# An encoder kernel in split float32: up projections by Strassen's seven products on halves

## The chip, the cores and the metric

The kernel runs on one core of a Trainium2 chip, in one launch. The core's engines are TensorE (PE: matmuls; PEld: their weight loads), VectorE (DVE), ScalarE (ACT), GpSimd (POOL) and SyncE (SP, which issues most DMAs). The metric is the device time in microseconds: the median of three runs before the change is 2168.96, from 2166.63 to 2170.75.

## The reference

Two layers of an encoder on 512 tokens with 1024 channels, followed by a last RMSNorm. Each layer is

```
x += 0.5 * swiglu(rms_norm(x, g1), Wgate1, Wup1, Wdown1)
z = rms_norm(x, gmix) @ W_in                # four mixers: neighbourhood, sliding-window,
y = concat of rms_norm of the 4 mixers      # latent and dilated attention
x += y @ W_out
x += 0.5 * swiglu(rms_norm(x, g2), Wgate2, Wup2, Wdown2)
x += sigmoid(rms_norm(x, gple) @ Wg) * (p @ Wp)

swiglu(u, Wgate, Wup, Wdown) = (silu(u @ Wgate) * (u @ Wup)) @ Wdown     # 1024 -> 2816 -> 1024
```

Everything is float32. There are four feed-forwards (two per layer), and the change is in them.

## The kernel before, in words

Activations lie with channels on the 128 partitions and the 512 tokens along the free axis, so x is eight tiles `x0` to `x7` of 128x512. A float32 product is done in three matmuls of a faster format: each operand is split into a high half, rounded to that format, and a low half, the rest (`split` for activations, lines 115 to 124; `pieces`, from line 150 on, for weights). `mm3y` (lines 194 to 203) issues, for each 128 rows of the contraction, high x high, high x low and low x high into one PSUM bank.

Weights come in tiles of 128x1024 (eight 128x128 blocks), 512 KB each, loaded by SP into `raw` (two buffers). A tile is cut in two pieces of four blocks: ACT writes the high half `wh` (L173) and DVE, in the mixers POOL, the low half `wl` (L175); each has three buffers. `plan` lists all weight tiles of the program in the order of use, and `take` hands out the next piece and prepares one more ahead. PE's and SP's instructions stand in the order in which the program writes them; the order of the other engines is laid out by a scheduler when the program is built, and is then fixed.

A feed-forward (`ffn`) has 22 gate tiles and 22 up tiles of 128 output channels, in two blocks of 11. Per tile f, `ffn` issues the gate's two pieces (24 matmuls of 512 columns into a bank `ps`), the up's two pieces (24 into a bank `s`), and `gated`: DVE multiplies the gate by the token's scale `rb`, ACT takes tanh, DVE makes silu (L276), multiplies by up (L277), and ACT and DVE split the result into `hs`. After a block follow eight down tiles with 8 + 3 blocks each, and DVE adds them to x (L316, L317). In the second block each finished x tile goes through `feed`: ACT and DVE write the split of x times the norm's gain (`act`, L122, L123) for the next stage, ACT squares x and POOL adds the squares (L216). The scale itself (`rstat`, `rspread`: four narrow matmuls, DVE, POOL, four transposes) is asked for after the first gate and up tile.

A mixer ends in `out` (inside `mix`): eight output tiles, each added to x by DVE (L779) and fed. The last part of a layer, `ple`, ends in the same way with `ple_out` (L821 to L824).

Of the kernel before, what the change touches and what calls it, by code (L numbers as in the profile page):

```python
# [16 lines left out]
D = 1024  # L17
T = 512
KC = 8
FF = 22  # L20
HF = 11
# [13 lines left out]
class Encoder:  # L35
# [34 lines left out]

    def dense(self):
        return self.ps.tile([128, T], F32, tag="ps", name=self.nm("ps"), bufs=3)
# [8 lines left out]
    def setup(self):  # L81
# [8 lines left out]
        self.supply = self.pieces()  # L90
# [35 lines left out]
    def plan(self):  # L126
        a = self.a
        full = ((0, 4, 128), (512, 4, 128))
        for l in range(self.depth):
            for w in range(2):  # L130
                for half in range(2):
                    for f in range(HF):
                        for i in range(2):
                            yield a["ffn_gu"][l, w, half * HF + f, i], full
                    for m in range(KC):
                        yield a["ffn_d"][l, w, half, m][:, 0:8], full
                        yield a["ffn_d"][l, w, half, m][:, 8:HF], ((0, 3, 128),)
                if w == 0:
                    for i in range(M_END):
                        if i == M_DQ0:  # L140
                            for j in range(2):
                                yield a["w_up"][l, j], ((0, 2, 256), (512, 1, 256))
                        yield a["w_in"][l, i], full
                    for i in range(8):
                        yield a["w_out"][l, i], full
            for m in range(KC):
                yield a["ple"][l, m][:, 0:4], ((0, 4, 128),)
                yield a["ple"][l, m][:, 4:10], ((0, 3, 128), (384, 3, 128))

    def pieces(self):  # L150
        nc, a = self.nc, self.a
        first = True
        for src, cuts in self.plan():
            n = cuts[-1][0] + cuts[-1][1] * cuts[-1][2]
            raw = self.tile("raw", [128, 1024], F32, 2)
            src = src.rearrange("p k m -> p (k m)") if len(src.shape) == 3 else src
            if first:
                nc.sync.dma_start(raw[:, :512], src[:, :512])
                nc.sync.dma_start(self.x[0], a["x"][:, 0])
                nc.sync.dma_start(self.x[1], a["x"][:, 1])  # L160
                nc.sync.dma_start(self.x[2], a["x"][:, 2])
                nc.sync.dma_start(raw[:, 512:], src[:, 512:])
                for k in range(3, KC):
                    nc.sync.dma_start(self.x[k], a["x"][:, k])
                first = False
            else:
                nc.sync.dma_start(raw[:, :n], src)
            for o, k, m in cuts:
                c = k * m
                hi = self.tile("wh", [128, 512], F32R, 3)[:, :c]  # L170
                lo = self.tile("wl", [128, 512], F32R, 3)[:, :c]
                r = raw[:, o:o + c]
                nc.scalar.activation(hi, r, AF.Copy)  # L173
                eng = nc.gpsimd if self.mixing else nc.vector
                eng.tensor_tensor(out=lo, in0=r, in1=hi.bitcast(F32), op=ALU.subtract)  # L175
                yield (hi.rearrange("p (k m) -> p k m", k=k), lo.rearrange("p (k m) -> p k m", k=k))

    def take(self):
# [3 lines left out]
        if not self.ready:  # L182
            self.prep()
        return w

    def prep(self):
        w = next(self.supply, None)
        if w is not None:
            self.ready.append(w)
# [56 lines left out]
    def begin(self, l, off):  # L246
        self.norm = (l, off)
        self.nacc = self.acc()
        self.xn = []

    def feed(self, m, square=True):
# [3 lines left out]
        if l < self.depth:  # L255
# [9 lines left out]

    def squared(self, m):
# [3 lines left out]
    def gated(self, gp, up, rb, h):  # L270
# [6 lines left out]
        nc.vector.tensor_tensor(gr, gr, up, op=ALU.mult)  # L277
        self.split(h, gr)

    def ffn(self, l, w, nxt):  # L280
        nc, a = self.nc, self.a
        xs, acc, rb = self.xn, self.nacc, None
        for half in range(2):
            hs = [self.big() if f < 6 else self.keep() for f in range(HF)]
            held = None
            for f in range(HF):
# [693 lines left out]
```

## Time and profile before

| | |
|---|---|
| median of 3 runs | 2168.96 us (2166.63 to 2170.75) |
| span of the profiled execution, first to last instruction | 2163.3 us |
| time of that execution beside its span | not given; the median lies 5.7 us above the span |
| instructions | 25721 |
| PE, PEld, DVE, ACT, POOL busy | 98%, 79%, 56%, 43%, 13% |
| DMA | 195.38 MB, mean 90 GB/s |
| mean granted clock of TensorE | 0.994 of 2.4 GHz |

Busy times of PE are modelled: a matmul of 512 columns is shown with 0.39 us, though the next one starts 0.23 us after it. So paces are read from the starts of successive instructions in the timeline, not from the durations. On DVE and ACT, too, a following instruction can start a little before the one ahead has ended.

### The profile page before, as it was taken

How to read it: one execution, taken by the hardware profiler on the slowest of the kernel's cores; microseconds unless marked ns; L12 is line 12 of the kernel's file. 1: busy time of each engine (PE TensorE's matmuls, PEld its weight loads, DVE VectorE, ACT ScalarE, POOL GpSimd, SP SyncE). 2: the span in 40 equal slices, each digit the busy share in tenths (PEclk: the TensorE clock that was granted, in tenths of full speed). 3: DMA queues.
4: the chain of work that ended last, by engine and by line, in shares of the span. 5: the costliest groups of instructions: out<-in, count | busy, mean ns of one | idle time of the engine just before them, and what ended most of it. 6: DMA issues, size and time to landing. Idle time of an engine off the chain costs nothing.

```text
span 2163.3 us, 25721 instructions
## 1 busy us (share of the span) xinstructions
PE 2117.2 (98%) x9564; PEld 1718.6 (79%) x9564; DVE 1210.5 (56%) x1926; ACT 930.1 (43%) x1690; POOL 280.0 (13%) x230
## 2 busy tenths in 40 slices
PE   8999999999999999999999999999999999999997
PEld 6888888677778888888888888886777788888886
DVE  5444446567766444456654444555687654444554
ACT  4332334477754332333533233345677533233343
POOL 2000001444321000001100000025332200000011
PEclk9999999999999999999999999999999999999998
DMA  3232223212112222223322322232121122322322
GB/s 129 97 109 99 98 94 111 90 60 75 40 54 93 98 96 99 98 98 96 100 96 98 94 102 98 93 102 93 64 59 49 59 98 98 94 101 98 102 92 89
DMA packets 63358, 195.38 MB, mean 90 GB/s; under 512 B 7552, under 2 KB 15872, under 8 KB 63232
## 3 DMA queue, kind: packets, MB, share of 16 engines
q1 hardware_dynamic: 61808, 187.92, 26.0%
q0 software_dynamic: 1280, 5.77, 1.0%
q8 instruction: 75, 1.23, 0.2%
q14 instruction: 51, 0.42, 0.1%
q10 hardware_dynamic: 144, 0.05, 0.0%
HBM read 189.51 MB, written 2.10 MB: 89 GB/s over the span
## 4 chain that ended last, share of the span: by engine, by line
PE 92%; DVE 4%; ACT 2%; issue 1%; DMA 1%; POOL 0%; POOLq 0%; SPq 0%; DVEq 0%; ACTq 0%
PE ps L200 15%; PE ps L201 15%; PE ps L202 15%; PE s L201 13%; PE s L200 13%; PE s L202 13%; PE pv L455 2%; PE s L439 2%; PE s L398 2%; PE s L397 1%; DVE kl L343 1%; PE s L225 1%; PE s L236 0%; ACT tmp L326 0%; DVE PT L443 0%
## 5 line engine op out<-in xcount | busy, mean ns | idle before, releaser
L173 ACT ACTIVATE wh<-raw 128x512 fp32r<-128x512 f32 (+1 forms) x712 | 437.8, 615 | 971.2 <-PE ps L201 457.3
L175 DVE TENSOR_TENSOR wl<-raw,wh 128x512 fp32r<-128x512 f32 (+1 forms) x614 | 435.6, 710 | 405.6 <-ACT wh L173 399.0
L200 PE MATMUL ps<-act,wh 128*128 128x512 f32 x616 | 248.8, 404 | 6.1 <-ACT act L122 6.1
L216 POOL TENSOR_TENSOR acc<-acc,tmp 128x512 f32<-128x512 f32 x54 | 72.3, 1340 | 1365.4 <-ACT tmp L215 1365.0
L200 PE MATMUL ps<-big,wh 128*128 128x512 f32 x616 | 247.0, 401 | 0.0
L201 PE MATMUL ps<-act,wh 128*128 128x512 f32 x616 | 242.7, 394 | 3.3 <-DVE act L123 3.1
L202 PE MATMUL ps<-act,wl 128*128 128x512 f32 x616 | 242.1, 393 | 0.0
L202 PE MATMUL ps<-big,wl 128*128 128x512 f32 x616 | 240.6, 391 | 0.0
L201 PE MATMUL ps<-big,wh 128*128 128x512 f32 x616 | 240.3, 390 | 0.0
L200 PE MATMUL s<-act,wh 128*128 128x512 f32 x520 | 202.4, 389 | 0.0
L200 PE MATMUL s<-big,wh 128*128 128x512 f32 x520 | 202.4, 389 | 0.0
L202 PE MATMUL s<-act,wl 128*128 128x512 f32 x520 | 202.3, 389 | 0.0
L202 PE MATMUL s<-big,wl 128*128 128x512 f32 x520 | 202.3, 389 | 0.0
L201 PE MATMUL s<-big,wh 128*128 128x512 f32 x520 | 202.3, 389 | 0.0
L201 PE MATMUL s<-act,wh 128*128 128x512 f32 x520 | 202.3, 389 | 0.0
L175 POOL TENSOR_TENSOR wl<-raw,wh 128x512 fp32r<-128x512 f32 (+1 forms) x98 | 127.4, 1300 | 286.6 <-ACT wh L173 286.4
L200 PEld LDWEIGHTS ps<-act,wh 128*128 128x128 f32 x616 | 116.7, 189 | 30.1 <-ACT act L122 6.4
L201 PEld LDWEIGHTS ps<-act,wh 128*128 128x128 f32 x616 | 116.7, 189 | 28.5 <-DVE act L123 7.3
L202 PEld LDWEIGHTS ps<-act,wl 128*128 128x128 f32 x616 | 116.6, 189 | 24.6
L202 PEld LDWEIGHTS ps<-big,wl 128*128 128x128 f32 x616 | 115.7, 188 | 24.7
L200 PEld LDWEIGHTS ps<-big,wh 128*128 128x128 f32 x616 | 116.0, 188 | 23.5 <-issue 1.1
L201 PEld LDWEIGHTS ps<-big,wh 128*128 128x128 f32 x616 | 116.2, 189 | 21.4
(172 smaller groups left out, 3373.1 us busy)
## 6 DMA issues: line engine op xcount, KB each, us to landing
raw<-in_ffn_gu SPq DMA_DIRECT2D x175, 512.0 KB, 3.5
raw<-in_ffn_d SPq DMA_DIRECT2D x64, 512.0 KB, 3.4
raw<-in_w_in SPq DMA_DIRECT2D x40, 512.0 KB, 3.5
raw<-in_ffn_d SPq DMA_DIRECT2D x64, 192.0 KB, 2.5
raw<-in_w_out SPq DMA_DIRECT2D x16, 512.0 KB, 3.5
raw<-in_ple SPq DMA_DIRECT2D x16, 384.0 KB, 3.0
raw<-in_ple SPq DMA_DIRECT2D x16, 256.0 KB, 2.6
nb<-in_na_bias POOLq DMA_DIRECT2D x8, 448.0 KB, 4.1
```

The costliest lines, as they stand in the source:

```text
L173: nc.scalar.activation(hi, r, AF.Copy)
L175: eng.tensor_tensor(out=lo, in0=r, in1=hi.bitcast(F32), op=ALU.subtract)
L200: nc.tensor.matmul(ps, lhsT=wh[:, k], rhs=x[:, 0], start=start and k == 0, stop=False)
L201: nc.tensor.matmul(ps, lhsT=wh[:, k], rhs=x[:, 1], start=False, stop=False)
L202: nc.tensor.matmul(ps, lhsT=wl[:, k], rhs=x[:, 0], start=False, stop=stop and k == last)
L216: eng.tensor_tensor(out=acc, in0=acc, in1=sq, op=ALU.add)
L225: nc.tensor.matmul(ss[:, t:t + 1], lhsT=acc[:, t * 128:(t + 1) * 128], rhs=self.ones, start=True, stop=True)
L343: nc.vector.tensor_tensor(out=kl[r], in0=u[r], in1=t[r, e].bitcast(F32), op=ALU.subtract)
L397: nc.tensor.matmul(s, lhsT=q[:, e, qs], rhs=k[0][:, e, k0:k1], start=True, stop=False)
L398: nc.tensor.matmul(s, lhsT=q[rows, e, qs], rhs=k[1][rows, k0:k1], start=False, stop=True)
L439: nc.tensor.transpose(tp[:, t * 128:(t + 1) * 128], h["P"][t][:, o:o + 128], self.ident)
L455: nc.tensor.matmul(pv[:, c], lhsT=vb, rhs=h["pt"][b][:, i, c], start=b == 0 and i == 0, stop=b == 3 and i == 1, skip_group_check=True)
```

## The change

For two neighbouring up tiles (an "up pair", 256 output channels) and the 512 tokens, the product W^T x is cut in halves in three directions: the eight tiles of x in those with even and odd number, the output channels in two tiles, the tokens in two halves of 256. Strassen's scheme in the variant with seven products then needs sums of weight halves (`factors`: four sums on DVE per pair), sums of activation halves (`combos`: made once per feed-forward, for each two x tiles, and split like the others into `pp` tiles), seven products (`product`: 4 x 3 matmuls of 256 columns each) and additions of the results. X1 to X4 add into one PSUM bank, Z1 and Z2 into another, Y is alone; after each step `seven` reads the bank on ACT or DVE into the up tiles `u`. `feed` writes x times gain first (ACT, L307 of the changed kernel) and splits that.

`ORDER` says how the pair's seven pieces (s) and the two gate tiles' four pieces (d) follow one another; the first pair of a feed-forward has `ORDER0`, and there the scale is asked for after the first two gate pieces. Two pieces instead of one are prepared ahead in the feed-forwards. Blocks are 12 and 10 tiles, so the down tiles have 8 + 4 and 8 + 2 blocks. `raw` has four buffers, which now hold the tables and biases of the mixers as well, and the mixers' P and PT lie in `pp`.

```diff
-HF = 11
+HT = 256
+CUT = (0, 12, 22)
+S_STEPS = ("X1", "Z1", "X2", "Y", "X3", "Z2", "X4")
+ORDER, ORDER0 = "ssdssdssdsd", "ddssdssdsss"
...
+                    for f in range(c0, c1, 2):
+                        gu = a["ffn_gu"][l, w]
+                        s = self.factors(gu[f, 1], gu[f + 1, 1])
+                        d = self.slices((gu[f, 0], full), (gu[f + 1, 0], full))
+                        for c in ORDER if f else ORDER0:
+                            yield s if c == "s" else d
...
+    def factors(self, src1, src2):
+        a, b = self.load(src1), self.load(src2)
+        a11, a12, a21, a22 = a[:, 0:512], a[:, 512:1024], b[:, 0:512], b[:, 512:1024]
...
+        yield self.cut(a11, 4)
+        s1 = plus(a21, a22)
+        yield self.cut(s1, 4)
+        s2 = plus(s1, a11)
+        yield self.cut(s2, 4)
+        yield self.cut(a12, 4)
+        yield self.cut(plus(a11, a21), 4)
+        yield self.cut(plus(s2, a12), 4)
+        yield self.cut(a22, 4)
...
+            nc.scalar.activation(xg, self.x[m], AF.Copy, scale=self.g(l, off, m))
+            self.split(t, xg)
+            if m % 2:
+                self.tn.append(self.combos(self.xg))
...
+        nc.vector.tensor_tensor(out=f[:, 0:2], in0=q[:, 0::3], in1=q[:, 1:2].to_broadcast([128, 2, HT]),
+                                op=ALU.subtract)
+        nc.vector.scalar_tensor_tensor(f[:, 2], f[:, 0], -1.0, q[:, 3], op0=ALU.mult, op1=ALU.subtract)
+        nc.vector.scalar_tensor_tensor(f[:, 3], f[:, 2], -1.0, q[:, 2], op0=ALU.mult, op1=ALU.subtract)
+        for i in (0, 2):
+            t = self.pp().rearrange("p e (h t) -> p e h t", h=2)
+            nc.scalar.activation(t[:, :, 0], f[:, i:i + 2], AF.Copy)
+            nc.vector.tensor_tensor(out=t[:, :, 1], in0=f[:, i:i + 2], in1=t[:, :, 0].bitcast(F32), op=ALU.subtract)
...
+    def product(self, ps, w, right, start):
+        nc = self.nc
+        wh, wl = w
+        for k, x in enumerate(right):
+            for i, (v, e) in enumerate(((wh, 0), (wh, 1), (wl, 0))):
+                nc.tensor.matmul(ps, lhsT=v[:, k], rhs=x[:, e], start=start and k == i == 0,
+                                 stop=k == 3 and i == 2, skip_group_check=True)
...
+            self.product(ps, self.take(), self.right(name, xs, tn), name in ("X1", "Y", "Z1"))
+            if name == "X1":
+                nc.scalar.activation(u[:, 0, lo], ps, AF.Copy)
+            elif name == "Z1":
+                nc.scalar.activation(u[:, 1, hi], ps, AF.Copy, scale=-1.0)
+            elif name == "X2":
+                nc.scalar.activation(u[:, 0, hi], ps, AF.Copy)
+            elif name == "Y":
+                nc.vector.tensor_tensor(u[:, 0, lo], u[:, 0, lo], ps, op=ALU.add)
+            elif name == "X3":
+                nc.vector.tensor_tensor(u[:, 1, hi], u[:, 1, hi], ps, op=ALU.subtract)
+            elif name == "Z2":
+                nc.vector.tensor_tensor(u[:, 0, hi], u[:, 0, hi], ps, op=ALU.add)
+            else:
+                nc.scalar.activation(u[:, 1, lo], ps, AF.Copy, scale=-1.0)
...
-            raw = self.tile("raw", [128, 1024], F32, 2)
+        return self.tile("raw", [128, 1024], F32, 4)
...
-        p = self.tile("P", [128, T], F32, 8)
+        if t % 2 == 0:
+            h["Pp"] = self.pp(F32)
+        p = h["Pp"][:, t % 2]
...
-        pt = self.tile("PT", [128, 2, T], F32R, 3)
+        pt = self.pp()
...
-            nb = self.tile("nb", [128, 896], F32, 1)
+            nb = self.raw()[:, :896]
...
-        cos = self.tile("tab", [128, T], F32, 2)
-        sin = self.tile("tab", [128, T], F32, 2)
+        tab = self.raw()
+        cos, sin = tab[:, :T], tab[:, T:]
```

On PE, in an up tile before: two blocks of the contraction, three matmuls of 512 columns each (`s` is the up's bank, `act` the split x).

```order
L200 MATMUL s97_522<-act8_112,wh95_506 128x512
L201 MATMUL s97_522<-act8_112,wh95_506 128x512
L202 MATMUL s97_522<-act8_112,wl96_507 128x512
L200 MATMUL s97_522<-act11_119,wh98_523 128x512
L201 MATMUL s97_522<-act11_119,wh98_523 128x512
L202 MATMUL s97_522<-act11_119,wl99_524 128x512
```

And in the changed kernel, the first product of a pair, X1, and the start of Z1 (`pp` holds the split sums of activations; "x2" are two matmuls with the same weights):

```order
L369 MATMUL s387_2031<-act5_103,wh370_1983 128x256 x2
L369 MATMUL s387_2031<-act5_103,wl371_1984 128x256
L369 MATMUL s387_2031<-act11_122,wh370_1983 128x256 x2
L369 MATMUL s387_2031<-act11_122,wl371_1984 128x256
L369 MATMUL s387_2031<-act19_145,wh370_1983 128x256 x2
L369 MATMUL s387_2031<-act19_145,wl371_1984 128x256
L369 MATMUL s387_2031<-act25_164,wh370_1983 128x256 x2
L369 MATMUL s387_2031<-act25_164,wl371_1984 128x256
L369 MATMUL s391_2051<-pp9_116,wh373_2001 128x256 x2
L369 MATMUL s391_2051<-pp9_116,wl374_2002 128x256
L369 MATMUL s391_2051<-pp15_135,wh373_2001 128x256 x2
L369 MATMUL s391_2051<-pp15_135,wl374_2002 128x256
```

The same contraction now passes in seven shorter runs of 256 columns, each with its own cut weights.

On DVE, inside a block before: cuts of weights (L175) alternate with the gating (L273, L276, L277, L120).

```order
L273 TENSOR_TENSOR tmp404_2172<-ps392_2102,rb49_260 128x512
L175 TENSOR_TENSOR wl403_2157<-raw401_2154,wh402_2156 128x512
L276 SCALAR_TENSOR_TENSOR tmp404_2172<-tmp405_2174,tmp404_2172 128x512
L175 TENSOR_TENSOR wl408_2182<-raw401_2154,wh407_2181 128x512
L277 TENSOR_TENSOR tmp404_2172<-tmp404_2172,s398_2137 128x512
L175 TENSOR_TENSOR wl411_2200<-raw409_2197,wh410_2199 128x512
L120 TENSOR_TENSOR keep277_1475<-tmp404_2172,keep277_1475 128x512
L175 TENSOR_TENSOR wl414_2217<-raw409_2197,wh413_2216 128x512
```

And in the changed kernel, at the place where a pair's last pieces meet the next pair's sums. `wl399` is the cut of the second half of gate tile `raw388`; `raw417` and `raw418` are the next pair's two up tiles, and `raw418` is loaded into the buffer of `raw388` after that cut; L212 are the sums, L390 and L392 read PSUM, L354 is the gating's first product, and `wl411` and `wl413` are cuts that this pair still needs.

```order
L197 TENSOR_TENSOR wl399_2089<-raw388_2032,wh398_2088 128x512
L197 TENSOR_TENSOR wl403_2109<-y401_2106,wh402_2108 128x512
L390 TENSOR_TENSOR keep386_2030<-keep386_2030,ps400_2105 128x256
L197 TENSOR_TENSOR wl406_2128<-y404_2125,wh405_2127 128x512
L212 TENSOR_TENSOR y421_2225<-raw418_2206 128x512
L212 TENSOR_TENSOR y432_2273<-y421_2225,raw417_2204 128x512
L212 TENSOR_TENSOR y441_2327<-raw417_2204,raw418_2206 128x512
L354 TENSOR_TENSOR tmp407_2143<-ps395_2071,rb70_310 128x512
L212 TENSOR_TENSOR y444_2346<-y432_2273,raw417_2204 128x512
L197 TENSOR_TENSOR wl411_2151<-raw409_2148,wh410_2150 128x512
L392 TENSOR_TENSOR keep386_2030<-keep386_2030,s387_2031 128x256
L197 TENSOR_TENSOR wl413_2168<-raw369_1981,wh412_2167 128x512
```

The four sums of the next pair now stand ahead of a cut of this pair, and the first of them needs a tile whose load is issued four rows earlier.

On DVE at the end of the first mixer, before: the last two x tiles are added (L779), a weight piece is cut, and the splits' low halves are written (L123).

```order
L779 TENSOR_TENSOR x6_78<-x6_78,ps1213_5521 128x512
L175 TENSOR_TENSOR wl1237_5584<-raw1219_5546,wh1236_5583 128x512
L123 SCALAR_TENSOR_TENSOR act1216_5539<-x6_78,gain_70,act1216_5539 128x512
L779 TENSOR_TENSOR x7_79<-x7_79,s1218_5545 128x512
L175 TENSOR_TENSOR wl1240_5602<-raw1238_5599,wh1239_5601 128x512
L123 SCALAR_TENSOR_TENSOR act1222_5565<-x7_79,gain_70,act1222_5565 128x512
L216 TENSOR_TENSOR acc1189_5410<-acc1189_5410,tmp1223_5568 128x512
```

And in the changed kernel, from the last add to x (L914) to the low half of x7 (`act1350`); L326, L328, L329 and L334 are the sums of activations and their low halves.

```order
L914 TENSOR_TENSOR x7_79<-x7_79,s1346_6320 128x512
L197 TENSOR_TENSOR wl1374_6380<-raw1371_6375,wh1373_6379 128x512
L133 TENSOR_TENSOR act1343_6312<-keep1344_6313,act1343_6312 128x512
L328 SCALAR_TENSOR_TENSOR keep1336_6281<-keep1336_6281,keep1329_6250 128x256
L197 TENSOR_TENSOR wl1377_6398<-y1375_6395,wh1376_6397 128x512
L334 TENSOR_TENSOR pp1323_6225<-keep1321_6218,pp1323_6225 128x2x256
L334 TENSOR_TENSOR pp1337_6285<-keep1336_6281,pp1337_6285 128x2x256
L326 TENSOR_TENSOR keep1351_6344<-keep1344_6313 128x512
L264 TENSOR_TENSOR acc1304_6144<-acc1304_6144,tmp1354_6354 128x512
L329 SCALAR_TENSOR_TENSOR keep1336_6281<-keep1336_6281,keep1329_6250 128x256
L133 TENSOR_TENSOR act1350_6340<-keep1344_6313,act1350_6340 128x512
```

From the first add to x up to x7's low half there are 22 rows before and 43 now.

## Rows read from the trace of the kernel before

**Rows 1.** The page: busy us, share of span and instructions by engine.

```profile
PE 2117.2 (98%) x9564; PEld 1718.6 (79%) x9564; DVE 1210.5 (56%) x1926; ACT 930.1 (43%) x1690; POOL 280.0 (13%) x230
```

**Rows 2.** Windows: span, busy us (x) of PE, PEld, DVE, ACT, POOL, clock, DMA.

```profile
380.00:700.00 320.00, 309.01 (x1474) 239.88 (x1473) 218.06 (x389) 198.23 (x409) 109.01 (x87) 0.99 0.21 70
700.00:950.00 250.00, 250.00 (x1104) 207.02 (x1103) 118.68 (x180) 80.46 (x129) 0.00 (x0) 1.00 0.29 97
```

**Rows 3.** Timeline of PE in a feed-forward: start us, us, engine, line, out<-in, count.

```profile
667.09 0.39 PE L200 MATMUL ps<-act,wh 128*128 128x512 f32 x1
...
669.81 0.39 PE L200 MATMUL s<-act,wh 128*128 128x512 f32 x1
```

**Rows 4.** Timeline of PE in the first mixer.

```profile
420.05 0.51 PE L455 MATMUL pv<-PT,big 128*128 128x256 f32 x2
...
440.25 0.40 PE L455 MATMUL pv<-PT,big 128*128 128x256 f32 x2
440.48 0.60 PE L469 MATMUL s<-ident,tmp 128*128 128x128 f32 x4
```

**Rows 5.** Lines by shape, whole span: count | busy us, mean ns.

```profile
L443 DVE TENSOR_TENSOR PT<-s,PT 128x512 fp32r<-128x512 f32 x64 | 43.5, 685 | 20.3 <-ACT PT L442 20.2
...
L443 DVE TENSOR_TENSOR PT<-s,PT 128x256 fp32r<-128x256 f32 x32 | 13.4, 420 | 5.3 <-ACT PT L442 5.1
...
L173 ACT ACTIVATE wh<-raw 128x512 fp32r<-128x512 f32 x612 | 385.6, 630 | 844.1 <-PE ps L201 410.4 <-PE s L201 359.1 <-PE s L202 23.3
```

**Rows 6.** Timeline of DVE, two independent instructions.

```profile
20.32 1.28 DVE L175 TENSOR_TENSOR wl<-raw,wh 128x512 fp32r<-128x512 f32 x2
```

**Rows 7.** Timeline of a feed-forward: one cut, then the next load.

```profile
701.19 0.63 ACT L173 ACTIVATE wh<-raw 128x512 fp32r<-128x512 f32 x1 [1.20 <-PE ps L201]
...
701.85 0.69 DVE L175 TENSOR_TENSOR wl<-raw,wh 128x512 fp32r<-128x512 f32 x1 [1.14 <-ACT wh L173]
...
702.57 0.33 SPq L167 DMA_DIRECT2D raw<-in_ffn_gu  x1
```

**Rows 8.** DMA issues: KB each, median us to landing.

```profile
raw<-in_ffn_gu SPq DMA_DIRECT2D x175, 512.0 KB, 3.5
```

**Rows 9.** Timeline of the start: DVE, POOL and PE.

```profile
4.97 0.69 DVE L175 TENSOR_TENSOR wl<-raw,wh 128x512 fp32r<-128x512 f32 x1 [4.97 <-ACT wh L173]
...
11.72 7.48 DVE L123 SCALAR_TENSOR_TENSOR act<-x,gain,act 128x512 fp32r<-128x512 f32 x5
...
8.21 9.77 POOL L216 TENSOR_TENSOR acc<-acc,tmp 128x512 f32<-128x512 f32 x6 [6.89 <-ACT tmp L215]
...
19.86 0.40 PE L200 MATMUL s<-act,wh 128*128 128x512 f32 x1
```

**Rows 10.** Timeline of DVE and PE at the first mixer's end.

```profile
649.61 0.69 DVE L779 TENSOR_TENSOR x<-x,ps 128x512 f32<-128x512 f32 x1 [0.18 <-PE ps L202]
...
668.23 0.74 DVE L123 SCALAR_TENSOR_TENSOR act<-x,gain,act 128x512 fp32r<-128x512 f32 x1
...
669.36 0.39 PE L201 MATMUL ps<-act,wh 128*128 128x512 f32 x1
```

**Rows 11.** Lines by shape, DVE, 649.5 to 669 us.

```profile
L123 DVE SCALAR_TENSOR_TENSOR act<-x,gain,act 128x512 fp32r<-128x512 f32 x8 | 7.9, 1002 | 0.2 <-ACT act L122 0.2
L175 DVE TENSOR_TENSOR wl<-raw,wh 128x512 fp32r<-128x512 f32 x6 | 6.5, 1088 | 0.0
```

**Rows 12.** Timeline of DVE and PE at the second layer's start.

```profile
1082.24 0.69 DVE L823 SCALAR_TENSOR_TENSOR tmp<-tmp,ps 128x512 f32<-128x512 f32 x1
1082.97 0.69 DVE L824 SCALAR_TENSOR_TENSOR x<-tmp,x 128x512 f32<-128x512 f32 x1
...
1084.69 0.75 DVE L123 SCALAR_TENSOR_TENSOR big<-x,gain,big 128x512 fp32r<-128x512 f32 x1
...
1083.38 0.39 PE L200 MATMUL ps<-big,wh 128*128 128x512 f32 x1
...
1085.65 0.40 PE L201 MATMUL ps<-big,wh 128*128 128x512 f32 x1
```

More of the change, by code (lines that the diff above doesn't have):

```diff
@@ new lines, in plan, with each, load @@
+                pl = a["ple"][l, m]
+                yield from self.each((pl[:, 0:4], ((0, 4, 128),)), (pl[:, 4:10], ((0, 3, 128), (384, 3, 128))))
+    def each(self, *srcs):
+        g = self.slices(*srcs)
+        for _, cuts in srcs:
+            for _ in cuts:
+                yield g
+    def load(self, src):
+        nc, a = self.nc, self.a
+        raw = self.raw()
+        src = src.rearrange("p k m -> p (k m)") if len(src.shape) == 3 else src
+        if self.first:
+            nc.sync.dma_start(raw[:, :512], src[:, :512])
+            nc.sync.dma_start(self.x[0], a["x"][:, 0])
+            nc.sync.dma_start(self.x[1], a["x"][:, 1])
+            nc.sync.dma_start(self.x[2], a["x"][:, 2])
+            nc.sync.dma_start(raw[:, 512:], src[:, 512:])
+            for k in range(3, KC):
+                nc.sync.dma_start(self.x[k], a["x"][:, k])
+            self.first = False
+        else:
+            nc.sync.dma_start(raw[:, :src.shape[1]], src)
+        return raw
@@ new lines, in cut, with slices @@
+    def cut(self, r, k):
+        nc = self.nc
+        c = r.shape[1]
+        hi = self.tile("wh", [128, 512], F32R, 3)[:, :c]
+        lo = self.tile("wl", [128, 512], F32R, 3)[:, :c]
+        nc.scalar.activation(hi, r, AF.Copy)
+        eng = nc.gpsimd if self.mixing else nc.vector
+        eng.tensor_tensor(out=lo, in0=r, in1=hi.bitcast(F32), op=ALU.subtract)
+        return hi.rearrange("p (k m) -> p k m", k=k), lo.rearrange("p (k m) -> p k m", k=k)
+    def slices(self, *srcs):
+        for src, cuts in srcs:
+            raw = self.load(src)
+            for o, k, m in cuts:
+                yield self.cut(raw[:, o:o + k * m], k)
@@ L268, in squared, with gate @@
         self.square(self.nacc, self.x[m], m == 0, nc.vector if m == KC - 1 else nc.gpsimd)
[L270 removed]
+    def gate(self, gp, rb):
         nc = self.nc
@@ new lines, in seven @@
+    def seven(self, xs, tn, u):
+        nc = self.nc
+        bank = {}
+        lo, hi = slice(0, HT), slice(HT, T)
+        for name in S_STEPS:
+            b = name[0]
+            if b not in bank:
+                bank[b] = (self.dense() if b == "Y" else self.small())[:, :HT]
+            ps = bank[b]
+            self.product(ps, self.take(), self.right(name, xs, tn), name in ("X1", "Y", "Z1"))
[11 more added lines that the diff above has]
+                nc.vector.tensor_tensor(u[:, 0, hi], u[:, 0, hi], ps, op=ALU.add)
+            else:
+                nc.scalar.activation(u[:, 1, lo], ps, AF.Copy, scale=-1.0)
+            yield name
```

157 lines of the change are left out of this document (89 added, 68 removed).

## The prediction

> **What bounds the kernel now.** I read the page first. TensorE (PE) is busy 98% of the span, VectorE (DVE) 56% and ScalarE (ACT) 43% [rows 1]. A busy PE is not yet a PE at its pace, so I read its timeline inside a feed-forward stage: from 667.09 to 669.81 stand twelve 512-column matmuls back to back, 0.2267 us each, and the windows view shows no idle PE in such a stage [rows 2, 3]. So matmul columns are the price in the feed-forwards, and taking some away is worth its full time as long as nothing else ends later. Four places are different: the start of the program, and the starts of the three other feed-forwards, where PE takes what DVE has just finished.
>
> **What it removes and adds on PE.** Each of four feed-forwards has 22 up tiles of 24 matmuls with 512 columns: 2112 matmuls, 478.8 us at 0.2267. Seven products for each of 11 pairs, 12 matmuls of 256 columns each, make 3696. Their pace isn't shown in a long run. Bounds: half of 0.2267 is 0.1133 (418.9 us, a gain of 59.9); each matmul brings its own weight load, and where loads of 128 columns set the pace, four narrow matmuls at 440.48 take 0.60; one of a pair at 440.25 is shown with 0.40 - 0.115 = 0.285, and with that they stand (0.60 - 0.285)/3 = 0.105 apart, so the load alone stays under 0.1133; above, 0.121 would be a pace with 0.008 of friction (447.2, a gain of 31.6). The nearest rows are pairs of 256-column matmuls with own loads: from 440.25 to 440.48 two take 0.23, so 0.115 [rows 4]. I take 0.115: 425.0 us, **-53.8**. The 12/10 split keeps the 2112 down matmuls.
>
> **What it adds on DVE and ACT per pair.** Before, DVE does 16 instructions of 128x512 per pair (8 cuts, 8 of the gating), now 23 of them (11 cuts, 4 sums, 8) and 3 of 128x256. An instruction lasts 0.69, but independent ones follow each other every 0.60: two take 1.28 [rows 5, 6]. With 0.605, and 0.35 for half the columns (0.69 to 0.42 is the ratio of the durations), that is 15.0 us beside a PE that now needs 48 x 0.2267 + 84 x 0.115 = 20.5 us. ACT has 11 cuts, 4 of gating and 4 evacuations, at 0.63 [rows 5] 12 us. So neither is the bound on average; what counts is where a wait stands in DVE's fixed order.
>
> **Pair boundaries.** As the DVE order in the section on the change shows, the next pair's sums stand between the cuts of this pair, and the first, y421, needs raw418. That load takes the buffer of raw388, free after the cut wl399, only four rows earlier. Let t be when PE ends the first gate piece, which frees wl399's buffers (three deep). A cut follows at once: ACT 0.66, then DVE 0.69, and the load is issued when DVE ends [rows 7]: t+1.4. It lands 3.5 us later [rows 8], t+4.9. Then y421 and the dependent y432 (0.73 apart, as two dependent instructions stand [rows 12]), y441, the gate product, y444 and wl411 at 0.605: wl411 begins at t+8.05 and ends at t+8.74. PE meanwhile runs X2, Y, a gate piece, X3 and Z2: 4 x 1.38 + 2.72 = 8.24, and loads wl411 for the third matmul of the next piece at about t+8.47. So PE waits about 0.25 us, at 5 + 4 boundaries of each of four feed-forwards: 36 x 0.25 = **+9**. At a landing of 3.2 it is nothing; at 4.5 it is 1.3 each. Queued behind y421 on DVE are this pair's gate product, two evacuations and two cuts; the later ones have over 1 us to spare.
>
> **Starts of feed-forwards.** The new `combos` gives DVE, for each two tiles of x, one sum of 512, two of 256 and two cuts, and `feed` gives ACT a scaled copy.
> At the program's start DVE has, up to the low half of x7, 26 instructions of 512 and 6 of 256: 17.8 us. While GpSimd (POOL) adds squares (9.77 us for six), five DVE instructions took 7.48, 1.5 each where 0.605 is usual [rows 9]; six adds thus cost DVE about 5.6. From 4.97, with 1.9 of waiting for x1, that ends near 30.4, and the second gate piece, whose last matmuls need it, near 30.9, where it ended at 19.86 before [rows 9]: **+11**.
> At the end of a mixer 22 instructions, from the first add to x at 649.61 to the low half of x7 at 668.97, become 43 (37 of 512, 6 of 256): 24.5 us [rows 10]. Add what POOL's adds cost, 8 x (1.002 - 0.75) + 6 x (1.088 - 0.69) = 4.4, and 0.9 of idle time [rows 11]: ready at 649.6 + 29.8 = 679.4. PE needed it at 669.36 and had it 0.4 us earlier; now it waits 10. This happens twice: **+20**. ACT's 36 instructions there (about 20 us) are not later.
> At the second layer's first feed-forward the low half of x7 was ready at 1085.44 for a matmul at 1085.65 [rows 12]. Now a cut for the product Z1 stands before the add to x7 and waits until PE ends the first gate piece (1083.4): ACT and DVE 1.4, the add 0.7, the scaled copy 0.7, three DVE instructions and the low half, about 1088.7: **+3**. The sum of squares is asked for after two pieces instead of four, but DVE's add of it stands before that low half, so it isn't late.
> **Costed at nothing.** Scores' P and PT, masks and tables share buffers with weights: PE's order in the mixers is the same, and PE idles 11 us of 320 there [rows 2], so a gain or loss of 3 us each is the most I allow. Bytes moved are the same. X1 to X4 add into one PSUM bank, and each must be read before the next: between X1 and X2 stand Z1 and a gate piece (4.1 us), in a first pair only Z2 (1.38) between X3 and X4, but X4's cut comes later than X3's evacuation ends plus 0.4.
>
> **Sum:** -53.8 + 9 + 11 + 20 + 3 = -10.8 us. The profile's span is 2163.3 and no other time is given for that execution; the median of the runs is 2169.0, 5.7 more, which the change doesn't touch. Forecast: 2158.
>
> **Rivals.**
> 1. DVE's order hides the handovers better than my sums: half of the 34 us at the starts and nothing at boundaries. For it: POOL's adds may fall on instructions that wait anyway. Against it: the sums at the starts are of DVE's work alone. Time: 2169 - 53.8 + 17 = 2132.
> 2. Slower: the wait for raw418 in DVE's order decides. With 1.3 us per boundary (two loads close together) 36 x 1.3 = 47, so 2169 - 53.8 + 34 + 47 = 2196. It decides from 0.55 us on, where the gain is gone. Against it: the pair's first load is issued some 2.7 us before the second, and the median of 175 loads is 3.5 [rows 8].
> 3. A 256-column matmul takes 0.121: 2169 - 31.6 + 43 = 2180. For it, small matmuls have a larger share of what doesn't scale with columns; against it the rows at 0.115.
> 4. A weight load doesn't run under the matmul before it. Then a product matmul takes 0.105 + 0.1133 = 0.218 us, 3696 of them 807 us, and the time is 2169 + 328 + 43 = 2540. For it: at 420.05 two 256-column matmuls take 0.51 - 0.285 = 0.225 to the second's start [rows 4]. Against it: 512-column matmuls with own loads stand 0.2267 apart, less than 0.2133 of columns at 2.4 GHz and 0.105 of load together, and the 0.225 is seen after a wait alone, where the first load itself was late.
> The Trainium skill, page "TensorE: Matmul & The Clock Gate", section "The mechanism" (Part 3), says that weight loads overlap with matmuls in flight only when the row groups differ; all row groups here are the same, so it is the rule behind rival 4. By it the change is much slower; the trace disagrees with 0.2267.
> The same page, section "Back-to-back issue gap", gives about 81 ns per matmul at 128 columns and 131 at 512 in a stream of loads and matmuls. An estimate between them for 256 is 98, and by it the sum on PE would be 3696 x 0.098 - 2112 x 0.131 = +85 us. No row here supports it: 512 columns take 0.2267.
> 5. The mixers, with shared buffers, lose what is left: 2169 within a few us.
>
> **How the numbers follow.** Forecast case (2150 to 2167) 0.44, rival 1 0.21, rival 2 0.14, rival 3 0.13, rival 4 0.01, rival 5 0.07. Below 0.2% (4.3 us, about what a measurement of this kernel can tell) faster: rival 1 and 0.36 of the forecast case, 0.57. Same: 0.08 of the forecast case, 0.05 of rival 5 and 0.03 of rival 3 with a pace of 0.118, 0.16. Slower: the rest, 0.27. The range that leaves 2 in 10 out runs from just below rival 1 to a little over rival 3, 2130 to 2190; the forecast case alone is 2150 to 2167.
>
> **What would show it.** In the profile after: product matmuls 0.115 apart in a run; PE idle of about 10 us at each start of a second feed-forward, released by DVE's low half of x7; the second gate piece ending near 31 us; waits of 0.2 to 0.3 us for a cut wl once per pair, and DVE idle before y421 released by the load. A pace over 0.12, waits of a microsecond at pair boundaries, or no wait at the starts would make the forecast wrong.

## The result and the profile after

The changed kernel takes 2205.43 us (median of 4 runs, 2202.95 to 2210.77), the kernel before 2168.26 us: 37 us slower, a ratio of 1.0175 with a 95% interval of 1.0158 to 1.0191. The forecast was 2158, with 2190 as its upper end. The profiled execution of the changed kernel took 2210.8 us, span 2209.0; so against the span before (2163.3) there are 45.7 us to explain. By the medians it is 37: the executions of all later runs last 1.8 to 2.2 us longer than their spans, so by that the profiled one of the kernel before took about 2165, some 3 us under its median, while that of the changed kernel lies 5.3 above its own. The terms below are those of the two traces and together some 8 us too large for the medians; which of them hold that excess isn't shown.

The page's row of engines, to be read beside [rows 1]: PE's share has fallen from 98% to 96%, and its busy time has not fallen at all, although an eighth of the up tiles' columns is gone.

```profile
PE 2121.9 (96%) x11148; PEld 1784.7 (81%) x11148; DVE 1484.4 (67%) x2446; ACT 1087.1 (49%) x2062; POOL 286.7 (13%) x230
```

To see where, I cut the span into stretches, which end some 10 us behind a statistic (the narrow matmuls that sum the squares for the scale), and subtracted from each 0.2267 us per 512-column matmul [rows 3] and, in the trace after, 0.120 us per product matmul. What is left is time that PE lost:

| term | forecast | traces |
|---|---|---|
| PE, up tiles: 3696 x 0.120 - 2112 x 0.2267 | -53.8 | -35.3 |
| pair boundaries, four feed-forwards | +9 | +9.2 |
| start of the program | +11 | +15.7 |
| from a mixer's last statistic into the second feed-forward, twice | +20 | +14.4 and +14.8 |
| start of the second layer's first feed-forward | +3 | +8.9 |
| the two mixers before that point | 0, 3 each way | +7.6 and +9.8 |
| the rest | 0 | +0.8 |
| sum | -10.8 | +45.9 |

First the pace. PE's timeline after, in a feed-forward (columns as in [rows 3]): a group of two with the same weights and one more begin 0.36 us apart, so three product matmuls take 0.36 and one takes 0.120.

```profile
709.25 0.40 PE L369 MATMUL s<-pp,wh 128*128 128x256 f32 x2
709.48 0.28 PE L369 MATMUL s<-pp,wl 128*128 128x256 f32 x1
709.60 0.40 PE L369 MATMUL s<-pp,wh 128*128 128x256 f32 x2
...
710.68 0.40 PE L369 MATMUL ps<-act,wh 128*128 128x256 f32 x2
```

Then the way from the first mixer into the second feed-forward. DVE's timeline after, where [rows 10] show it before:

```profile
667.81 0.69 DVE L914 TENSOR_TENSOR x<-x,ps 128x512 f32<-128x512 f32 x1 [0.18 <-PE ps L250]
...
678.08 0.68 DVE L212 TENSOR_TENSOR y<-raw 128x512 f32<-128x512 f32 x1
...
683.23 1.17 DVE L197 TENSOR_TENSOR wl<-raw,wh 128x512 fp32r<-128x512 f32 x1
...
698.07 0.68 DVE L133 TENSOR_TENSOR act<-keep,act 128x512 fp32r<-128x512 f32 x1
```

From the first add to x to the end of x7's low half are 30.9 us; before they were 19.4, and I had forecast 29.8. PE over the same time:

```profile
680.08 0.39 PE L249 MATMUL s<-keep,wh 128*128 128x512 f32 x1
684.45 0.51 PE L250 MATMUL s<-keep,wl 128*128 128x512 f32 x1 [3.98 <-DVE wl L197]
684.78 0.60 PE L248 MATMUL s<-keep,wh 128*128 128x512 f32 x1
685.18 0.63 PE L249 MATMUL s<-keep,wh 128*128 128x512 f32 x1
...
694.52 0.50 PE L249 MATMUL ps<-act,wh 128*128 128x512 f32 x1 [1.34 <-DVE act L133]
694.86 0.39 PE L250 MATMUL ps<-act,wl 128*128 128x512 f32 x1
695.09 0.40 PE L248 MATMUL ps<-act,wh 128*128 128x512 f32 x1
698.80 0.80 PE L249 MATMUL ps<-act,wh 128*128 128x512 f32 x1 [3.32 <-DVE act L133]
...
702.17 0.63 PE L369 MATMUL s<-act,wh 128*128 128x256 f32 x2
702.60 0.41 PE L369 MATMUL s<-act,wl 128*128 128x256 f32 x1
702.81 0.63 PE L369 MATMUL s<-act,wh 128*128 128x256 f32 x2
```

Two things are to be seen. PE waits first for a weight cut of the mixer's own last tile (683.23 on DVE), which stands behind the sums in DVE's order, then 1.34 us for another x tile's low half, and at the end for x7's low half, as forecast. And after the first and the last of these waits it is slow: 512-column matmuls 0.43 us apart from 684.78 on, products 0.64 per three from 702.17 on, about twice the time. 0.43 us for 512 columns is the lower of the engine's two clocks, 1.2 GHz. After the wait of 1.34 us the pace stayed at 0.23. The granted clock of the three stretches with such waits (windows, columns as in [rows 2]):

```profile
657.30:709.00 51.70, 43.06 (x189) 35.33 (x188) 40.68 (x63) 28.96 (x53) 14.68 (x9) 0.90 0.17 53
1106.90:1128.20 21.30, 17.37 (x73) 14.29 (x73) 14.14 (x24) 9.80 (x18) 2.93 (x2) 0.76 0.16 51
1742.10:1794.60 52.50, 43.97 (x190) 35.35 (x189) 41.42 (x64) 29.17 (x52) 13.11 (x9) 0.87 0.16 53
```

and of the first of them in the kernel before, where PE was never idle and had its full clock:

```profile
639.10:696.00 56.90, 56.90 (x264) 47.28 (x263) 37.95 (x54) 26.78 (x46) 11.46 (x9) 1.00 0.27 93
```

Pair boundaries. DVE's and PE's timelines after, at the largest of these waits:

```profile
83.14 0.69 DVE L197 TENSOR_TENSOR wl<-y,wh 128x512 fp32r<-128x512 f32 x1
85.86 0.69 DVE L212 TENSOR_TENSOR y<-raw 128x512 f32<-128x512 f32 x1 [2.02 <-DMA raw<-in_ffn_gu]
...
88.99 0.68 DVE L197 TENSOR_TENSOR wl<-raw,wh 128x512 fp32r<-128x512 f32 x1
```

```profile
88.25 0.40 PE L249 MATMUL ps<-act,wh 128*128 128x512 f32 x1
89.73 0.50 PE L250 MATMUL ps<-act,wl 128*128 128x512 f32 x1 [1.08 <-DVE wl L197]
```

It is the chain that the prediction followed: the load, y421's row (L212), four more rows, the cut, PE. DVE waits for that load at 40 of 44 pairs, 31.1 us in all, but PE is reached at few of them: six of its waits there exceed 0.13 us (3.3 us together, the largest 1.25), 23 more make 2.2, and the rest of the 9.2 is spread in steps of about 0.04 and less.

Last the mixers. The group rows of two lines, whole span (count | busy us, mean ns | idle time just before, and what ended it), after:

```profile
L574 PE MATMUL s<-ident,pp 128*128 128x128 f32 x416 | 69.4, 281 | 5.1 <-DVE ne L539 4.7 <-ACT pp L545 0.4
L525 PE MATMUL s<-big,big 128*128 128x512 f32 x16 | 7.2, 452 | 4.2 <-DMA big<-pp 3.7 <-ACT pp L545 0.5
```

and the first of these lines before, where its tiles are `P`:

```profile
L439 PE MATMUL s<-ident,P 128*128 128x128 f32 x416 | 68.6, 278 | 1.5 <-ACT P L410 1.5
```

Transposes of P now wait for scores, and the latent heads' scores wait longer for a DMA that copies the latent key (waits of 3.7 and 3.4 us, before one of 1.9).

### The profile page after: what moved, and what is told of

It is laid out like the page before. It is cut to its first block, busy times and chain, and to the rows that moved or that the text cites. A ratio compares the mean times of both kernels' runs of the same rounds, so it can differ in the third digit from the quotient of the medians.

```text
span 2209.0 us, 29889 instructions
## 1 busy us (share of the span) xinstructions
PE 2121.9 (96%) x11148; PEld 1784.7 (81%) x11148; DVE 1484.4 (67%) x2446; ACT 1087.1 (49%) x2062; POOL 286.7 (13%) x230
## 4 chain that ended last, share of the span: by engine, by line
PE 85%; DVE 9%; ACT 3%; issue 2%; DMA 1%; POOL 0%; POOLq 0%; SPq 0%; DVEq 0%; ACTq 0%
PE s L369 17%; PE ps L248 15%; PE ps L249 14%; PE ps L250 14%; PE s L249 5%; PE s L248 4%; PE s L250 4%; PE ps L369 3%; PE pv L590 2%; PE s L574 2%; PE s L531 2%; DVE wl L197 1%; PE s L273 1%; PE s L530 1%; DVE y L212 1%
## 5 line engine op out<-in xcount | busy, mean ns | idle before, releaser
L195 ACT ACTIVATE wh<-raw 128x512 fp32r<-128x512 f32 (+2 forms) x668 | 409.4, 613 | 743.2 <-PE ps L249 418.5
L197 DVE TENSOR_TENSOR wl<-raw,wh 128x512 fp32r<-128x512 f32 x570 | 401.8, 705 | 241.2 <-ACT wh L195 230.6
L249 PE MATMUL ps<-act,wh 128*128 128x512 f32 x632 | 252.0, 399 | 15.6 <-DVE act L133 15.6
L248 PE MATMUL ps<-act,wh 128*128 128x512 f32 x632 | 257.3, 407 | 8.7 <-ACT act L132 8.7
L369 PE MATMUL s<-pp,wh 128*128 128x256 f32 x1408 | 263.2, 285 | 0.0
L248 PE MATMUL ps<-big,wh 128*128 128x512 f32 x632 | 256.4, 406 | 2.9 <-ACT big L132 2.9
L249 PE MATMUL ps<-big,wh 128*128 128x512 f32 x632 | 250.2, 396 | 5.6 <-DVE big L133 5.6
L369 PEld LDWEIGHTS s<-pp,wh 128*128 128x128 f32 x1408 | 230.7, 194 | 10.0
L369 PE MATMUL s<-pp,wl 128*128 128x256 f32 x704 | 200.7, 285 | 0.0
L197 DVE TENSOR_TENSOR wl<-y,wh 128x512 fp32r<-128x512 f32 x176 | 121.8, 692 | 66.3 <-ACT wh L195 60.7
L195 ACT ACTIVATE wh<-y 128x512 fp32r<-128x512 f32 x176 | 111.4, 633 | 103.5 <-PE s L369 66.2
L369 PEld LDWEIGHTS s<-pp,wl 128*128 128x128 f32 x704 | 136.3, 194 | 0.0
```

Of the source, the lines that this page charges most:

```text
L248: nc.tensor.matmul(ps, lhsT=wh[:, k], rhs=x[:, 0], start=start and k == 0, stop=False)
L249: nc.tensor.matmul(ps, lhsT=wh[:, k], rhs=x[:, 1], start=False, stop=False)
L369: nc.tensor.matmul(ps, lhsT=v[:, k], rhs=x[:, e], start=start and k == i == 0, stop=k == 3 and i == 2, skip_group_check=True)
```

## The experiments

"The kernel before" in each is a run on the same chip. The changed kernel was not run again: what is said against it uses its 2205.43 from above, and the medians of the kernel before differ by 1.5 us from session to session. With one run of a kernel there is no interval, and its time is good to about 4 us, the spread of the others.

### What a matmul of 256 columns costs (e2_256, e2_384)

In the kernel before, up tiles with parts of `c = (0, 256, T)`, and then `c = (0, 384, T)`:

```diff
-                self.full(up, xs)
+                self.parts(up, xs)
...
+        for q in (0, 4):
+            wh, wl = self.take()
+            for o, e in zip(c, c[1:]):
+                for k in range(4):
+                    x = xs[q + k]
+                    for i, (v, j) in enumerate(((wh, 0), (wh, 1), (wl, 0))):
+                        nc.tensor.matmul(ps[:, o:e], lhsT=v[:, k], rhs=x[:, j, o:e], start=q == k == i == 0,
...
```

Each part of a bank is started for itself while the other part's sum is open, which changes what is computed; number and shape of the instructions are as stated.

Expected, 256: 

> The kernel before, with every up matmul of 512 columns cut in two of 256 with their own weight loads; the product is the same, 2112 more matmuls. Theory A, a matmul takes its columns at 2.4 GHz plus 0.0133 us whatever its width: 0.120 each, 2112 x 0.0133 = 28 us more, 2197. Rival B, the 0.115 of the prediction: 2112 x 0.0033 = 7 us more, 2175. Rival C, the changed kernel's 0.120 is due to its order (other weights after every third matmul): then 0.1133 to 0.117 here, 2168 to 2183.

Expected, 384: 

> The same with 384 and 128 columns. Theory A, 0.0133 us per matmul whatever its width: 0.1733 + 0.0667 = 0.240 for the two, the same 28 us more, 2197. Rival, a weight load of 128 columns takes at least about 0.105 to 0.12 and doesn't shrink with the matmul: 0.1733 + 0.11 = 0.283 for the two, 2112 x 0.057 = 120 us more, 2288; then 256 columns at 0.120 would be close to this floor.

Measured: 2195.84 and 2299.16 us against 2169.00 (one run each): +27 and +130. PE's timeline with 256 columns, then with 384 and 128:

```profile
702.40 0.40 PE L217 MATMUL s<-act,wh 128*128 128x256 f32 x2
702.64 0.28 PE L217 MATMUL s<-act,wl 128*128 128x256 f32 x1
702.76 0.40 PE L217 MATMUL s<-act,wh 128*128 128x256 f32 x2
```

```profile
743.09 0.52 PE L217 MATMUL s<-act,wh 128*128 128x384 f32 x2
743.45 0.34 PE L217 MATMUL s<-act,wl 128*128 128x384 f32 x1
743.63 0.51 PE L217 MATMUL s<-act,wh 128*128 128x384 f32 x2
743.98 0.33 PE L217 MATMUL s<-act,wl 128*128 128x384 f32 x1
744.15 0.51 PE L217 MATMUL s<-act,wh 128*128 128x384 f32 x2
...
744.95 0.39 PE L217 MATMUL s<-act,wh 128*128 128x128 f32 x2
745.18 0.27 PE L217 MATMUL s<-act,wl 128*128 128x128 f32 x1
745.29 0.39 PE L217 MATMUL s<-act,wh 128*128 128x128 f32 x2
```

So 0.36 for three of 256 columns, 0.54 and then 0.52 for three of 384, 0.34 for three of 128. The 0.120 holds outside the seven products too: theory A for the first. For widths of 256 and more the pace is the columns at 2.4 GHz plus 0.013 to 0.02 us; 128 columns do not go under about 0.112, so there theory A failed (+28 us) and the rival with the floor stands (+120). 256 columns lie 0.008 above it. The statistics' matmuls have one column and a weight load of 128, and in the kernel before they, too, start 0.112 us apart (eight from 675.25 on): the columns are not what takes this time. Every one of these matmuls has a load of its own, so that it is the load, and not another fixed cost, isn't shown.

### What the mixers lost (e1_storage, e6_raw, e7_rings, e9_after_rings)

The changed kernel puts P, PT and the latent key into `pp`. e1 makes all its storage changes, and nothing else, in the kernel before:

```diff
+    def raw(self):
+        return self.tile("raw", [128, 1024], F32, 4)
+    def pp(self, dt=F32R):
+        return self.tile("pp", [128, 2, T], dt, 8)
...
-        p = self.tile("P", [128, T], F32, 8)
+        if t % 2 == 0:
+            h["Pp"] = self.pp(F32)
+        p = h["Pp"][:, t % 2]
...
-        pt = self.tile("PT", [128, 2, T], F32R, 3)
+        pt = self.pp()
...
-        kpe = self.tile("kpe", [128, 2, T], F32R, 1)
+        kpe = self.pp()
...
```

Expected: 

> The kernel before, with the changed kernel's storage for the mixers alone (raw of four buffers that also holds tables and biases; P, PT and the latent key in pp tiles): no seven products, no sums, blocks of 11. The changed kernel's mixers, up to the first add to x, are about 7.6 us longer each. Theory A, the shared buffers make these waits: both mixers 6 to 8 us longer, feed-forwards unchanged, about 2182. Rival B, the waits come from elsewhere (two pieces prepared ahead, another order on DVE and ACT that the feed-forwards leave behind): mixers within 1.5 us of before, about 2168.

Measured: 2182.50 against 2169.00, ratio 1.0054 (1.0038 to 1.0071). From statistic to statistic the mixers are 7.6 and 9.9 us longer than before, in the changed kernel 7.6 and 9.7. The rows are those of the changed kernel, to a tenth:

```profile
L447 PE MATMUL s<-ident,pp 128*128 128x128 f32 x416 | 69.2, 280 | 5.1 <-DVE ne L412 4.7 <-ACT pp L418 0.4
...
L398 PE MATMUL s<-big,big 128*128 128x512 f32 x16 | 7.0, 437 | 4.2 <-DMA big<-pp 3.7 <-ACT pp L418 0.5
```

Not all of this is waiting. The two mixers in e1 and then in the kernel before (windows, columns as in [rows 2]):

```profile
384.40:647.10 262.70, 247.91 (x1171) 188.20 (x1172) 176.66 (x332) 169.34 (x360) 97.56 (x78) 0.97 0.20 65
1458.20:1722.30 264.10, 249.59 (x1173) 188.98 (x1173) 176.54 (x332) 169.33 (x360) 97.74 (x78) 0.97 0.20 64
```

```profile
384.00:639.10 255.10, 244.11 (x1172) 185.81 (x1172) 177.44 (x332) 168.54 (x360) 97.36 (x78) 0.99 0.19 63
1450.20:1704.30 254.10, 242.65 (x1172) 185.14 (x1172) 177.37 (x332) 168.63 (x360) 97.41 (x78) 0.99 0.19 63
```

PE is idle some 7 us longer and busy some 11 us longer, at a lower granted clock. Of its 512-column matmuls there, 47 stand 0.40 to 0.46 us from the next, before 15: that is 6.4 of the 17.6 us, and the same slow pace that the result shows at the starts.

e6 keeps the `raw` half of that change and gives P, PT and the key their own tiles back. Expected: 

> The kernel before with the first half of the storage change alone: raw has four buffers that also hold the mixers' tables and biases; P, PT and the latent key keep tiles of their own. The whole storage change cost 7.7 us in the first mixer and 10 in the second. Theory A, a bias or table that waits for one of the four buffers makes the waits: 12 to 18 us of it are here, 2181 to 2186. Rival B, P and PT in one ring of eight make them: under 5 us here, 2168 to 2174.

Measured: 2164.53 against 2169.11 (one run). Theory A fell: the tables and biases in `raw` cost nothing that this run shows, which leaves `pp`.

e7 keeps everything and splits that ring, with the same bytes:

```diff
-    def pp(self, dt=F32R):
-        return self.tile("pp", [128, 2, T], dt, 8)
+    def pp(self, dt=F32R, ring=0):
+        return self.tile("pp%d" % ring, [128, 2, T], dt, (4, 3, 1)[ring])
...
-        pt = self.pp()
+        pt = self.pp(ring=1)
...
-        kpe = self.pp()
+        kpe = self.pp(ring=2)
```

Expected: 

> The kernel before with the whole storage change, but the eight pp tiles as three rings (four for P, three for PT, one for the latent key) instead of one of eight; the same bytes. With one ring it took 2182.5, with the raw half of the change alone 2164.5. Theory A, one ring makes P, PT and the key wait for each other's release: with rings of their own nothing is lost, 2163 to 2170. Rival B, the loss is from two P halves in one tile, which is freed only when both have been read: it stays, 2178 or more.

Measured: 2165.57 against 2167.94 (one run): theory A, it is the one ring. The added waits are gone, and those that remain (1.5 and 1.9 us) are as long as before the change:

```profile
L447 PE MATMUL s<-ident,pp 128*128 128x128 f32 x416 | 68.8, 279 | 1.5 <-ACT pp L418 1.5
...
L398 PE MATMUL s<-big,big 128*128 128x512 f32 x16 | 6.7, 420 | 2.1 <-DMA big<-pp 1.9
```

Then the same split in the changed kernel, whose eight sums of activations take four, three and one tile of the rings. Expected: 

> The changed kernel with the three pp rings and nothing else changed. Theory A, one ring costs it what it cost the kernel before when the storage was changed alone, 7.6 us in the first mixer and 9.8 in the second: 2205.4 - 17.4 = 2188, 2184 to 2192. Rival B, the changed kernel's mixers lose through the order that the feed-forwards leave on DVE, so rings help little: 2198 or more.

Measured: 2193.34 against 2167.57, ratio 1.0119 (1.0102 to 1.0136): 12 us under the changed kernel, between the two theories. In the trace the mixers are 8.5 and 8.1 us shorter than in the changed kernel (the second still 1.6 longer than before), and the span, 2192.2, is 16.8 us shorter; the profiled execution of the changed kernel lies 5 us above its median, so by medians it is less.

### What the late starts come from (e3_nocombos, e5_nosums, e4_late)

e3 takes plain halves of x in place of the sums of activations:

```diff
-            if m % 2:
-                self.tn.append(self.combos(self.xg))
...
+        if l < self.depth and off in (G_FFN1, G_FFN2) and m % 2:
+            self.tn.append([v.rearrange("p e (h t) -> p h e t", h=2) for v in self.xn[-2:]])
```

Expected: 

> The changed kernel without the sums of activations and their splits: the products take plain halves of the split x instead (this changes what is computed). ACT's scaled copy of x stays. Theory A, DVE's work on these sums makes the late starts: of the excess at the mixers' ends and the starts of the second feed-forwards, 14 us each, nearly all goes, of the program's start about 10 and of the second layer's start about 3, so about 2205 - 41 = 2164. Rival B, the scaled copy on ACT that now precedes each split, or the order of the work, makes them: under 10 us come back, 2196 or more.

Measured: 2175.82 (one run), 30 us less than the changed kernel; 41 were expected. From statistic to statistic the way out of the first mixer takes 33.0 us, in the changed kernel 42.5, and before 30.7 to the same point. So the sums make 9.5 of the 11.8 there; about 2 are of the rest. In stretches like those of the first table the four starts lose 14 us more than before the change, where they lost 54: the forecast of 41 for them holds, and theory A with it. The mixers, though, lose 4 us more here and the pair boundaries 1, and 5 are those by which the profiled execution of the changed kernel lies above its median.

e5 leaves out the four sums of weights:

```diff
         def plus(u, v):
-            t = self.ytile()
-            self.nc.vector.tensor_tensor(out=t, in0=u, in1=v, op=ALU.add)
-            return t
+            return u
```

Expected: 

> The changed kernel without the four sums of weights per pair: the cuts read plain weight halves instead (this changes what is computed). Theory A, as the trace after has it: boundaries cost about 2 us in a feed-forward, 3 in the first, so 7 to 10 us in all come back, 2196 to 2199. Rival B, DVE's load of 4 x 0.6 us per pair also sets the starts or the mixers: more than 15 us, below 2190. Rival C, the boundary waits are of the loads alone and stay: within 3 us of 2205.

Measured: 2184.61 (one run), 21 us less than the changed kernel: rival B. In the trace the four feed-forwards behind their first statistic are 6.0, 2.4, 2.4 and 1.2 us shorter, and the starts up to that statistic another 11.6: the first pair's sums (L212 at 678.08 in the rows above) stand between the splits of x, so this work, too, is paid for at the start.

e4 does the first pair of each feed-forward as before and makes the sums of activations from x while PE works on that pair:

```diff
+    def first_pair(self, l, w, xs, acc, hs):
+        for e in range(2):
...
+            self.mm3(up, self.take(), xs[0::2], stop=False)
+            self.mm3(up, self.take(), xs[1::2], start=False)
...
+            for j in range(4):
+                self.tn.append(self.combos(l, off, j))
```

Expected: 

> The changed kernel with the first pair of each feed-forward done as before (gate, up, gate, up; 512 columns), and the scaled copies and sums of activations made during that pair, from x; the seven products from the second pair on. Theory A, the late starts come from DVE's work on the sums ahead of the first gate tile: 2 x 14 us at the mixers' ends, about 3 at the second layer's start and some 12 at the program's start go, and 4 x 0.8 us of PE's gain with them: 2205 - 43 + 3 = 2165, between the kernel before and 1% under the changed one at the least. Rival B, the same work only waits elsewhere (the second pair is late): no more than 10 us come back, 2195.

Measured: 2179.78 against 2169.11, ratio 1.0052 (1.0035 to 1.0069): 26 us less than the changed kernel, not 40. In stretches like those of the first table the starts still lose 20 us, and the mixers 20 instead of 17. DVE's timeline at the program's start shows why the starts do:

```profile
8.68 1.30 DVE L325 TENSOR_TENSOR keep<-keep 128x512 f32<-128x512 f32 x1 [0.38 <-ACT keep L322]
9.91 1.83 DVE L136 SCALAR_TENSOR_TENSOR act<-x,gain,act 128x512 fp32r<-128x512 f32 x1
11.67 1.50 DVE L327 SCALAR_TENSOR_TENSOR keep<-keep,keep 128x256 f32<-128x256 f32 x1
...
21.04 1.40 DVE L136 SCALAR_TENSOR_TENSOR act<-x,gain,act 128x512 fp32r<-128x512 f32 x2
```

The sums (L325, L327) were written later in the program, but the scheduler moved them up between the splits of x (L136).

### A version that beats both (e8_best, e10_onering)

e4 with the three rings, the scaled copies pinned behind what ACT has by then (written after the first gate tile), and the second pair in `ORDER0`:

```diff
-            nc.scalar.activation(xg[:, e], self.x[2 * j + e], AF.Copy, scale=self.g(l, off, 2 * j + e))
+            self.tc.keep_in_program_order(
+                nc.scalar.activation(xg[:, e], self.x[2 * j + e], AF.Copy, scale=self.g(l, off, 2 * j + e)))
```

Expected: 

> The changed kernel with the first pair of each feed-forward as before, with the three rings, with the sums of activations pinned behind the first gate tile on ACT, and with the gate's first two pieces ahead of the products in the second pair. With the late sums alone it took 2179.8. Theory A, what it still lost there are 18 us of one ring in the mixers and about 15 us of sums that the scheduler had put ahead of x's splits: 2179.8 - 18 - 12 = 2150, with PE's gain of 4 x 8 us against the kernel before nearly whole. Rival B, the second pair now waits for its sums, 3 us or more in each feed-forward: 2162 or more.

Measured: 2143.52 (2142.08 to 2144.46) against 2167.94, ratio 0.9890 (0.9872 to 0.9908): 24 us under the kernel before and 62 under the changed one, and 6 under theory A's 2150. The way from the mixer into the feed-forward (windows) is without idle time on PE and at full clock, although DVE is busy 49.81 us of it:

```profile
635.10:692.00 56.90, 56.90 (x275) 47.80 (x274) 49.81 (x79) 36.16 (x63) 11.96 (x9) 1.00 0.25 84
```

and the one ring again in this version. Expected: 

> The version of 2143.5 (first pair as before, sums of activations behind the first gate tile, three rings) with the one ring of eight pp tiles again. Theory A, the ring's 17 to 18 us and the starts add up: 2161, 2157 to 2165, and the starts alone then are 2205.4 - 2161 = 44. Rival B, the rings also carried the sums of activations, so more comes back: 2168 or more.

Measured: 2156.94 against 2167.57 (one run): theory A by its lower edge. The ring costs 13 us here. What the late sums (with the first pair as before), the pin and `ORDER0` save together with one ring is 48, from 2205.4 to 2156.9; of that the pin and `ORDER0` make 23 (from e4's 2179.8), and no run tells these two apart.

## Why the prediction was wrong

**The pace on PE was mis-sized, by 18.5 us.** The prediction took 0.115 from a pair of rows that are 0.23 us apart [rows 4]; with two matmuls and two digits this can't tell 0.115 from 0.120. [Rows 3] had the answer: 0.2267 less 0.2133 of columns are 0.0133 that half a matmul pays in full, 0.1067 + 0.0133 = 0.120. Rival 3 had 0.121. It did not decide alone: with its 18.5 the forecast would have been 2177, inside the range.

**"Scores' P and PT, masks and tables share buffers with weights ... 3 us each is the most I allow" failed.** The mixers cost 17.4 us in the trace; by the medians e1 puts the same storage at 13.5. e1, e6, e7 and e9 show the cause: P, PT and the latent key in one ring of eight. "PE's order is the same" was true and beside the point, since waits were in the buffers, and slow matmuls behind them. The prediction looked at idle shares of the kernel before, which can't show a ring that does not exist yet. Which tile in the ring waited for which release isn't shown; only that separate rings of the same bytes end the waits.

**The starts were right in place and in DVE's sum, and too small: the term had the wait and nothing behind it.** 34 us forecast, 53.8 in the trace. The idle time itself was not larger than forecast: in the two ways out of a mixer PE is idle 8.6 and 8.5 us (51.70 less 43.06 and 52.50 less 43.97 in the windows above), where 10 were forecast. x7's low half came 30.9 us after the first add, 29.8 by the forecast; the program's second gate piece ended at 32.6, forecast 31. Missing was what follows a wait: matmuls at half the pace. Counted by their pace (0.40 to 0.46 us for 512 columns, 0.19 to 0.24 for 256), the four starts have 29 and 79 of them, 13 us, where before there were 4. The rows of the statistics, 1.70 us for eight where 0.95 is usual, add 0.75 each. At the second layer's first feed-forward the low half was also 2 us later than forecast. e3 shows that the sums of activations make most of the starts (40 of 54 us), e5 that those of weights hold back some as well (18 of 54 in the same stretches, 12 of it up to the statistic); the two overlap, as they make more than 54 together. In e8 all but about 2 us is gone.

**Pair boundaries were right, 9 against 9.2 us,** and the chain was the one described; but its form was not. Not 36 waits of 0.25, but many near zero and a few up to 1.25, so that the sums agree is luck. Rival 2, which put its slower outcome here, was wrong in its cause, though its 2196 lies nearest to the result.

**The forecast's sum fell between its rivals.** Each was priced alone: pace, mixers and starts failed together and in one direction, 18.5 + 17.4 + 19.8 = 55.7 us, which is nearly all of the 56.5 between -10.8 and +45.7 (between the forecast 2158 and the median there are 47). Rival 5 had named the mixers, but with the 11 us that bring 2158 to 2169, and alone.

Rival 4 fell with the product rows: 0.120 us per matmul with a load of its own, less than a load of 0.105 and 0.107 of columns one after the other. The Trainium skill, page "TensorE: Matmul & The Clock Gate", section "The mechanism" (Part 3), has a line by which loads overlap with matmuls in flight only where row groups differ; here they are the same, and the trace disagrees. The sentence ahead of it there also lets a load run ahead into the background weight buffer, which would fit these rows; no run here shows which buffer a load takes. The estimate of 98 ns from its section "Back-to-back issue gap" isn't reached either: 120.

## What to carry to other kernels

A pace is to be taken from a long run, and its part that doesn't shrink with the matmul has to be separated before the matmul is halved: here half the columns cost 53% of the time. Work that is moved to an engine with idle time is free only where nobody waits for that engine next; it belongs behind the work that others wait for, and where a scheduler orders it, writing it later isn't enough (e4): look in the trace at where it landed. Buffers that are merged to save space are better left in rings of their own: here one ring of eight cost 13 us and the same bytes in three rings nothing. And a wait of PE is to be priced with the slow matmuls behind it.

## What was not expected of the hardware

Waits of PE cost more than themselves here: after the idle gaps of 3.98 and 3.32 us (the timelines above) the following 512-column matmuls stood 0.43 us apart instead of 0.2267, with a mean granted clock of 0.76 to 0.90 over those stretches. At the program's start the pace is the same,

```profile
28.00 0.63 PE L248 MATMUL ps<-act,wh 128*128 128x512 f32 x1
28.43 0.63 PE L249 MATMUL ps<-act,wh 128*128 128x512 f32 x1
```

but the granted clock of the first 40 us reads 1.00 there; which of the two is right at that place stays open. A matmul with a weight load of its own did not come under about 0.112 us in a stream at the higher clock, with 128 columns or with one, so that per matmul a cut from 256 to 128 columns saves 0.008.
